# A decoder trunk on one core: the RWKV inverse on four 64x64 quadrants, rotary tables in steps, new mixing waits and a branch hint

## The chip, the cores and the metric

The kernel runs on one core of one Trainium2 chip. The metric is the device time of one execution in microseconds (us). The kernel before took 2006.41 us as the median of three runs (2005.33 to 2008.68). Engines are named as in the profile: PE (TensorE matmul) and PEld (its weight loads), DVE (VectorE), ACT (ScalarE), POOL (GpSimd) and SP (which issues the DMAs).

## The reference

The reference is a hybrid decoder trunk with two layers on 256 tokens of width 1024, in float32:

```
h = rmsnorm(x);  u = h @ W_in
x = x + (sum_m sigmoid(gate_m) * (mixer_m(u_m) @ P_m)) @ W_o      # SSD, NSA, RWKV-7, sliding-window attention
x = x + FFN(rmsnorm(x))          # layer 0: dense SwiGLU; layer 1: top-2 of 8 experts
x = x + sigmoid(x @ W_pg) * (p @ W_pp)
```

The RWKV mixer is a recurrence over tokens. For eight heads of size 64 it computes S_t = S_{t-1}(diag(w_t) - kk_t^T (a_t kk_t)) + v_t^T k_t and o_t = S_t r_t. The sliding-window mixer rotates its queries and keys by sine and cosine of position times frequency (rotary tables).

## The kernel before

**Main stream.** All large products go through one stream of units (`run_units`). A unit loads a piece of a weight from HBM (`raw`), splits it into a high part H (a cast on ACT, L318) and a low part L = raw - H (DVE, L321, and a quarter of the columns on POOL, L323), and then PE runs three matmuls for each product: H by H, L by H, H by L (L362 to L364). Results are called `fm` (features on partitions), `tokm` (tokens on partitions), `gu` and `dn` (expert layers).

**Side chains.** The mixers are Python generators (`rwkv_half`, `ssd`, `nsa`, `swa`, also `rope_tables` and `cast`). They are put on a list `side`, and each call of `tick` (L223), which stands between pieces of the main stream, lowers their counters; one whose counter has run out emits its instructions up to its next `yield`. How many ticks a step waits is read from the table `WAITS` by the generator's name and the step's number, else from the number that the generator yields. So WAITS decides where a chain's instructions stand among the main stream's. Nothing is reordered afterwards: every engine takes its instructions in the order in which they were emitted.

**The RWKV inverse.** Tokens are handled in chunks of 64. A "half" of the RWKV mixer (`rwkv_half`, four of them: two for each layer) has four heads and four chunks, 16 matrices of 64x64, held as 128 partitions by eight units: one matrix in partitions 0 to 63 and one in 64 to 127 of each unit. It needs the inverse of a unit triangular matrix for each, and builds it by doubling in five levels (L850 to L860). Level by level it forms `m1` = LO^T X (16 products, which the profile shows as 32 instructions, two for each float32 product), copies it to M1 on ACT, forms `dx` = XT^T M1 and `dxt` = M1^T XT, and adds them to X (L857) and to XT, the transpose of X (L859). The last level needs `dxt` alone. Each 64x64 product takes one quadrant of PE's 128x128 array: its rows are the partitions of the operands, its columns the partitions of the result. Before the change both are the same half, so the two products of a unit take the two quadrants on the diagonal:

```
ps = psb(name)
for u in range(8):
    for sl in HD:                                        # the two halves of the partitions
        mm(u3(ps)[sl, u], u3(lhs)[sl, u], rhs(sl, u), start=True, stop=True)
```

The start value X is a transpose of LO on PE (`d0`) plus the identity, and XT is LO plus the identity, made on POOL (L846). After the inverse a scan over four chunks follows (`rhs`, `sap`, `stp`, `op`); `sap` uses XT (L881).

**Rotary tables.** `rope_tables` (L518) emits ten POOL instructions in a row (L525 to L535), then waits once, then three on DVE (L537 to L539) and two on ACT. `cast` (L169) turns constants to bfloat16 on POOL.

**The branch.** The last part of the expert layer holds code for an expert with over 128 tokens. `tc.If(Z.most > P)` (L1996) lets every engine jump over it; with these inputs it is not needed. Behind the branch stands the scatter of the last expert (`last_scatter`, L1908): ACT casts yeH (L371), then PE forms `sct` (L1918).

Of the kernel before, what the change touches and what calls it, by code (L numbers as in the profile page):

```python
# [48 lines left out]
def _consts():  # L49
# [37 lines left out]
    for k, v in cols.items():  # L87
# [10 lines left out]


WAITS = {  # L100
# [19 lines left out]
}  # L120


def trunk_kernel(tc, I, out, dbg=None, upto=99):
# [38 lines left out]
    def late_consts(place):  # L162
        stages = []
        for c in range(NC32, NCST, 512):
            w = min(512, NCST - c)
            stages.append((c - NC32, w, place("stage")))
            nc.sync.dma_start(stages[-1][2][:, :w], I["consts"][:, c:c + w])

        def cast():  # L169
            yield 8.0  # L170
            for c, w, t in stages:
                nc.gpsimd.tensor_copy(cstb[:, c:c + w], t[:, :w])
        return cast

    def K(name):
        o, w = COFF[name]
        return cst[:, o:o + w] if o < NC32 else cstb[:, o - NC32:o - NC32 + w]
# [217 lines left out]
    def dma2(dst, src):  # L395
        nc.sync.dma_start(dst, src)
# [121 lines left out]
    def rope_tables(place):  # L518

        pool = nc.gpsimd  # L520
        pos, scr = place("pos"), place("scr")
        posi = pos.bitcast(I32)[:, 0:S]
        ang, nn = scr[:, 0:S], scr[:, S:2 * S]
        dma2(posi, I["positions"].to_broadcast([P, S]))
        pool.tensor_copy(ang, posi)  # L525
        pool.tensor_scalar(ang, ang, K("invf"), None, ALU.mult)
        magic = 12582912.0
        pool.tensor_scalar(nn, ang, 1.0 / (2 * math.pi), magic, ALU.mult, ALU.add)
        pool.tensor_scalar(nn, nn, magic, None, ALU.subtract)
        c1 = 6.28125  # L530
        c2 = 0.0019350051879882812
        c3 = 2 * math.pi - c1 - c2
        for c in (c1, c2, c3):
            pool.tensor_scalar(cosT, nn, -c, None, ALU.mult)
            pool.tensor_tensor(ang, ang, cosT, ALU.add)  # L535
        yield 12.0
        ts(ang, ang, math.pi, -math.pi, ALU.min, ALU.max)  # L537
        stt(nn, ang, -1.0, ang, ALU.mult, ALU.max)
        ts(nn, nn, -1.0, math.pi / 2, ALU.mult, ALU.add)  # L539
        yield 2.0  # L540
        act(sinT, ang, AF.Sin)
        act(cosT, nn, AF.Sin)
# [9 lines left out]
    def mixing(l, after):  # L552
# [176 lines left out]
        def rwkv_half(hf):  # L729
# [75 lines left out]
                        mm(u3(ps)[sl, u], u3(src)[sl, u], ident[sl, sl], start=True, stop=True)  # L805
                return ps

            def per_unit(lhs, rhs, name):
                ps = psb(name)
                for u in range(8):  # L810
                    for sl in HD:
                        mm(u3(ps)[sl, u], u3(lhs)[sl, u], rhs(sl, u), start=True, stop=True)
                return ps

            tok = []
            LT, Gka, Gbr, Gkr = (R(n) for n in ("LT", "Gka", "Gbr", "Gkr"))
            for src, da, dr in ((beta, LT, Gbr), (kap, Gka, Gkr)):
# [15 lines left out]
            bt, kpt, Vt = tok  # L833


            def off_diagonal(lev):
                LO = Z.mxr.tile([P, 512], F32, tag="LO", name="LO", bufs=2)
                nc.gpsimd.tensor_tensor(u3(LO), u3(LT), bmask("lv", lev * 64), ALU.mult)
                return LO
# [1 line left out]
            X, XT, M1 = R("X"), R("XT"), R("M1")  # L841
            LO = off_diagonal(0)
            yield
            ps = turn_units(LO, "d0")
            tt(u3(X), u3(ps), bmask("eye64"), ALU.add)
            nc.gpsimd.tensor_tensor(u3(XT), u3(LO), bmask("eye64"), ALU.add)  # L846
            LO = off_diagonal(1)
            yield
            for lev in range(1, 6):
                ps = per_unit(LO, lambda sl, u: u3(X)[sl, u], "m1")  # L850
                nc.scalar.copy(M1, ps)
                if lev < 5:
                    LO = off_diagonal(lev + 1)
                yield 1.6
                if lev < 5:
                    psx = per_unit(XT, lambda sl, u: u3(M1)[sl, u], "dx")
                    tt(X, X, psx, ALU.add)  # L857
                ps = per_unit(M1, lambda sl, u: u3(XT)[sl, u], "dxt")
                tt(XT, XT, ps, ALU.add)  # L859
                yield 2.2  # L860

# [2 lines left out]
            for c in range(4):  # L864
# [2 lines left out]
                    yield  # L867
                ps = psb("rhs")[:, :P]
                for q in range(2):
                    for sl in HD:  # L870
                        o = ps[sl, q * 64:q * 64 + 64]
                        mm(o, u3(Gka)[sl, u(q)], u3(Vt)[sl, u(q)], start=True, stop=c == 0)
                        if c:
                            mm(o, AR[sl, u(q), 0], St[sl, q], start=False, stop=True)
# [2 lines left out]
                yield  # L877
                ps = psb("sap")[:, :P]
                for q in range(2):
                    for sl in HD:  # L880
                        mm(ps[sl, q * 64:q * 64 + 64], u3(XT)[sl, u(q)], rh[sl, q], start=True, stop=True)  # L881
                sa = Z.mxr.tile([P, 2, 64], F32, tag="sa", name="sa", bufs=2)
                vec.tensor_copy(sa, ps.rearrange("p (q v) -> p q v", q=2))
                yield
# [491 lines left out]
        def swa():  # L1376
            mxa = Z.mxa
            qs = query_tile()
            ks = key_tile("kr")
            for n in range(5):  # L1380
                yield from until(F(f"rr{n}."))
                yield 2.0
                raw = rr[n]
                rp = psb("rotp")[:, :S]
                mm(rp, K("rot"), raw, start=True, stop=True)
                t = mxa.tile([P, S], F32, tag="rt", name="rtmp", bufs=2)
                tt(t, rp, sinT, ALU.mult)
                nc.gpsimd.tensor_tensor(raw, raw, cosT, ALU.mult)
                tt(t, t, raw, ALU.add)
                if n:  # L1390
                    split_to(qs[0][:, n - 1], qs[1][:, n - 1], t)
                else:
                    for g in range(2):
                        split_to(ks[0][HD[g], g], ks[1][HD[g], g], t[HD[g]])
            nsk = mxa.tile([P, 4, 2], F32, tag="nsk", name="nsk")
            ts(nsk, Z.snk.rearrange("p (g r) -> p r g", g=2), -1.0, None, ALU.mult)
            branch_out("swa", Z.mxa, 1)
            def use(PT, r):
                o = psb("so")[:, :S]
                pv(o, 256, PT, True, True)  # L1400
                head_out("swa", r, o)

            yield from until(F("nsa"))
            yield from attn_pipe([(qs, ks, r, None, True, nsk[:, r], lambda PT, r=r: use(PT, r)) for r in range(4)])
            flags.add(F("swa"))
# [329 lines left out]
    def moe(l, Z):  # L1735
# [252 lines left out]

        def load_most():
            Z.most = nc.values_load(Z.mxi[0:1, 0:1], min_val=0, max_val=S)  # L1990
            tc.mark_branch_hint_location("overflow")

        experts(0)

        def overflow():
            with tc.If(Z.most > P, label="overflow"):  # L1996
                keep = list(stream)
                stream.clear()
                experts(P)
                mine = list(stream)  # L2000
                stream[:] = keep
                with tc.tile_pool(name="ovr", bufs=2) as r2, tc.tile_pool(name="ovs", bufs=2) as s2:
                    run_units(mine, Slots(r2, 2, s2, 2))
            if f"xffn{l}" in dbg:
                for i in range(2):
                    nc.sync.dma_start(dbg[f"xffn{l}"][i], x[:, i])
# [44 lines left out]
```

## Time and profile before

| | |
|---|---|
| median of 3 runs | 2006.41 us (2005.33 to 2008.68) |
| profiled execution | 2005.13 us, of which the span is 2003.3 us |
| PE busy | 1938.6 us, 97% of the span |
| DVE, ACT, POOL busy | 77%, 59%, 56% |
| mean granted clock of PE | 0.989 |

Mixing takes about the first 440 us for layer 0 and from about 690 to 1117 us for layer 1; the dense layer lies between, the experts after. The page's "busy" of PE overlaps neighbouring matmuls, since they are pipelined; how long a group holds PE is read from the start of the group to the start of the next one.

### The profile page before, as it was taken

The numbers are of one execution on the slowest core, as the hardware profiler recorded it, in microseconds if no ns is written. First come the engines' busy times: TensorE is split into PE (matmuls) and PEld (weight loads), VectorE is DVE, ScalarE is ACT, GpSimd is POOL, SyncE is SP. The second block draws the span as 40 slices with busy tenths as digits, with TensorE's granted clock in tenths as the row PEclk, the third lists the DMA queues.
The fourth block names the chain that finished last, engine by engine and source line by source line (L and its number), as shares of the span: only waits on it lengthen the run. The fifth ranks groups of instructions, "written<-read, shape, count | busy, mean of one in ns | idle before, by whom it ended". The sixth has DMA issues, their size and how long they took to land. (4 is left out here: it accounts for less than half of the span.)

```text
span 2003.3 us, 37459 instructions
## 1 busy us (share of the span) xinstructions
PE 1938.6 (97%) x13236; PEld 1606.8 (80%) x13236; DVE 1533.7 (77%) x2432; ACT 1176.9 (59%) x1786; POOL 1120.4 (56%) x976
## 2 busy tenths in 40 slices
PE   7999999999999899999999999999999999999997
PEld 6798897778999788878777777778777877787775
DVE  6475756766555666656666589999999999999996
ACT  5333445545444443334455567777877787778773
POOL 4543254454555254414354666777767767777773
PEclk9999999999999999999999999999999999999998
DMA  7322464457665453228354889999999999999973
GB/s 202 96 75 82 111 146 137 117 160 216 187 189 166 115 133 93 76 85 163 102 146 137 280 270 354 313 330 351 360 354 331 347 362 357 328 349 362 354 255 107
DMA packets 419441, 435.78 MB, mean 218 GB/s; under 512 B 67876, under 2 KB 355624, under 8 KB 419240
## 3 DMA queue, kind: packets, MB, share of 16 engines
q1 hardware_dynamic: 419240, 433.26, 69.1%
q8 instruction: 106, 1.74, 0.4%
q14 instruction: 95, 0.78, 0.1%
HBM read 432.13 MB, written 1.05 MB: 216 GB/s over the span
## 5 line engine op out<-in xcount | busy, mean ns | idle before, releaser
L323 POOL TENSOR_TENSOR L<-raw,H 128x256 fp32r<-128x256 f32 (+1 forms) x794 | 950.8, 1207 | 808.7 <-ACT H L318 608.8
L321 DVE TENSOR_TENSOR L<-raw,H 128x768 fp32r<-128x768 f32 (+1 forms) x792 | 933.3, 1207 | 169.2 <-ACT H L318 166.7
L318 ACT CAST H<-raw 128x1024 fp32r<-128x1024 f32 x794 | 828.6, 1047 | 227.0 <-issue 44.8
L362 PE MATMUL gu<-H,GH 128*128 128x512 f32 x704 | 286.5, 407 | 0.1
L363 PE MATMUL gu<-L,GH 128*128 128x512 f32 x704 | 279.3, 397 | 0.5 <-DVE L L321 0.5
L364 PE MATMUL gu<-H,GL 128*128 128x512 f32 x704 | 278.1, 395 | 1.1 <-DVE GL L375 1.1
L364 PE MATMUL dn<-H,aL 128*128 128x512 f32 x440 | 173.9, 395 | 1.6 <-DVE aL L372 1.6
L363 PE MATMUL dn<-L,aH 128*128 128x512 f32 x440 | 174.5, 397 | 0.0
L362 PE MATMUL dn<-H,aH 128*128 128x512 f32 x440 | 174.3, 396 | 0.2 <-ACT pj L1576 0.2
L362 PE MATMUL fm<-hTH,H 128*128 128x256 f32 x560 | 166.9, 298 | 0.0
L363 PEld LDWEIGHTS gu<-L,GH 128*128 128x128 f32 x704 | 132.5, 188 | 41.1 <-DVE L L321 15.0
L363 PE MATMUL fm<-hTL,H 128*128 128x256 f32 x560 | 157.8, 282 | 0.0
L364 PE MATMUL fm<-hTH,L 128*128 128x256 f32 x560 | 157.5, 281 | 0.0
L364 PEld LDWEIGHTS gu<-H,GL 128*128 128x128 f32 x704 | 132.4, 188 | 29.0 <-DVE GL L375 2.7
L362 PEld LDWEIGHTS gu<-H,GH 128*128 128x128 f32 x704 | 132.3, 188 | 27.3 <-ACT GH L374 0.6
L362 PE MATMUL tokm<-H,hTH 128*128 128x512 f32 (+1 forms) x320 | 139.1, 435 | 4.4 <-ACT H L318 4.4
L363 PE MATMUL tokm<-L,hTH 128*128 128x512 f32 (+1 forms) x320 | 126.8, 396 | 5.6 <-POOL L L323 4.0
L364 PE MATMUL tokm<-H,hTL 128*128 128x512 f32 (+1 forms) x320 | 126.4, 395 | 0.0
L362 PEld LDWEIGHTS fm<-hTH,H 128*128 128x128 f32 x560 | 106.4, 190 | 5.9 <-issue 2.7
L363 PEld LDWEIGHTS fm<-hTL,H 128*128 128x128 f32 x560 | 106.4, 190 | 0.2
L364 PEld LDWEIGHTS fm<-hTH,L 128*128 128x128 f32 x560 | 106.2, 190 | 0.0
L363 PEld LDWEIGHTS dn<-L,aH 128*128 128x128 f32 x440 | 82.6, 188 | 23.8 <-DVE L L321 7.6
(507 smaller groups left out, 3520.2 us busy)
## 6 DMA issues: line engine op xcount, KB each, us to landing
raw<-moe_w_gate SPq DMA_DIRECT2D x341, 256.0 KB
raw<-moe_w_up SPq DMA_DIRECT2D x341, 256.0 KB
raw<-moe_w_down SPq DMA_DIRECT2D x169, 512.0 KB
raw<-w_in SPq DMA_DIRECT2D x126, 512.0 KB
raw<-ffn_w_gate SPq DMA_DIRECT2D x22, 512.0 KB
raw<-ffn_w_up SPq DMA_DIRECT2D x22, 512.0 KB
raw<-ffn_w_down SPq DMA_DIRECT2D x22, 512.0 KB
raw<-w_in SPq DMA_DIRECT2D x32, 256.0 KB
```

The costliest lines, as they stand in the source:

```text
L318: nc.scalar.copy(H[:, :n], raw[:, :n])
L321: tt(L[:, :m], raw[:, :m], H[:, :m], ALU.subtract)
L323: nc.gpsimd.tensor_tensor(L[:, m:n], raw[:, m:n], H[:, m:n], ALU.subtract)
L362: mm(o, l[0], r[0], start=start, stop=False)
L363: mm(o, l[0], r[1], start=False, stop=False)
L364: mm(o, l[1], r[0], start=False, stop=stop)
```

## The change

`m1` now goes to the other half of the columns, so M1 and XT lie in the partitions opposite to X. `dx` and `dxt` are emitted product by product in turn, so that a unit's four products name four different quadrants. `d0` is joined by `d0t`, a product with the identity as weights, which puts LO's copy in the other half; XT is then made on DVE from PSUM. `rhs` and `sap` follow the halves. The rotary tables, `cast` and `swa` have further `yield`s, and WAITS is set anew. The branch tests the opposite condition and has a hint.

```diff
 WAITS = {
+    'cast0': {0: 12, 1: 6, 2: 1, 3: 1, 4: 1},
+    'rope_tables0': {0: 10, 3: 7, 5: 3, 6: 4},
...
@@ rope_tables
         dma2(posi, I["positions"].to_broadcast([P, S]))
+        yield 2.5
         pool.tensor_copy(ang, posi)
         pool.tensor_scalar(ang, ang, K("invf"), None, ALU.mult)
+        yield 1.2
...
         for c in (c1, c2, c3):
             pool.tensor_scalar(cosT, nn, -c, None, ALU.mult)
             pool.tensor_tensor(ang, ang, cosT, ALU.add)
-        yield 12.0
+            yield 1.2
@@ rwkv_half
-            ps = turn_units(LO, "d0")
+            ps, pst = psb("d0"), psb("d0t")
+            for u in range(8):
+                for h, sl in enumerate(HD):
+                    mm(u3(ps)[sl, u], u3(LO)[sl, u], ident[sl, sl], start=True, stop=True)
+                    mm(u3(pst)[HD[1 - h], u], ident[sl, sl], u3(LO)[sl, u], start=True, stop=True)
             tt(u3(X), u3(ps), bmask("eye64"), ALU.add)
-            nc.gpsimd.tensor_tensor(u3(XT), u3(LO), bmask("eye64"), ALU.add)
+            tt(u3(XT), u3(pst), bmask("eye64"), ALU.add)
...
-                ps = per_unit(LO, lambda sl, u: u3(X)[sl, u], "m1")
+                        mm(u3(ps)[HD[1 - h], u], u3(LO)[sl, u], u3(X)[sl, u], start=True, stop=True)
...
+                psx = psb("dx") if lev < 5 else None
+                ps = psb("dxt")
+                for u in range(8):
+                    for h in range(2):
+                        if lev < 5:
+                            mm(u3(psx)[HD[h], u], u3(XT)[HD[1 - h], u], u3(M1)[HD[1 - h], u], start=True, stop=True)
+                        mm(u3(ps)[HD[1 - h], u], u3(M1)[HD[1 - h], u], u3(XT)[HD[1 - h], u], start=True, stop=True)
                 if lev < 5:
-                    psx = per_unit(XT, lambda sl, u: u3(M1)[sl, u], "dx")
                     tt(X, X, psx, ALU.add)
-                ps = per_unit(M1, lambda sl, u: u3(XT)[sl, u], "dxt")
                 tt(XT, XT, ps, ALU.add)
@@ swa
                 tt(t, t, raw, ALU.add)
+                yield 1.2
                 if n:
                     split_to(qs[0][:, n - 1], qs[1][:, n - 1], t)
@@ load_most, overflow
-            tc.mark_branch_hint_location("overflow")
+            tc.mark_branch_hint_location("overflow", "LikelyTaken", engines=list(mybir.ALL_ENGINES))
-            with tc.If(Z.most > P, label="overflow"):
+            with tc.If(Z.most <= P, label="overflow", preferred_fallthrough_block=False) as fits:
+                pass
+            with fits.Else():
```

On PE, at a level of the first half, the kernel before runs one product kind after the other (16 source products each):

```order
L362 MATMUL fm<-hTH,H 128x256
L363 MATMUL fm<-hTL,H 128x256
L364 MATMUL fm<-hTH,L 128x256
L812 MATMUL dx<-M_828,XT 64x64 x16
L812 MATMUL dxt<-XT,M_828 64x64 x16
L362 MATMUL fm<-hTH,H 128x256
```

The changed kernel has the same 32 in turn; six of them with the main matmuls ahead:

```order
L368 MATMUL fm<-hTH,H 128x256
L369 MATMUL fm<-hTL,H 128x256
L370 MATMUL fm<-hTH,L 128x256
L870 MATMUL dx<-M_814,XT 64x64
L871 MATMUL dxt<-XT,M_814 64x64
L870 MATMUL dx<-M_814,XT 64x64
L871 MATMUL dxt<-XT,M_814 64x64
L870 MATMUL dx<-M_814,XT 64x64
L871 MATMUL dxt<-XT,M_814 64x64
```

The number of main matmuls ahead of a level is the same at most levels; only the turn within the group is new.

On POOL, in layer 0 where the rotary tables are made, the kernel before has all ten instructions ahead of a low part L that the main stream needs (`kp`, `AR` and `kap` belong to RWKV):

```order
L775 TENSOR_TENSOR kp<-kp,k 128x512
L781 TENSOR_TENSOR AR<-r,Dd 128x8x64
L525 CAST scr<-pos 128x256
L526 TENSOR_SCALAR scr<-scr,cst 128x256
...
L534 TENSOR_SCALAR cosT<-scr 128x256
L535 TENSOR_TENSOR scr<-scr,cosT 128x256
L323 TENSOR_TENSOR L<-raw,H 128x192
L787 TENSOR_TENSOR kap<-kp,inv 128x512
L323 TENSOR_TENSOR L<-raw,H 128x192
```

The changed kernel puts four low parts ahead and spreads the rest:

```order
L784 TENSOR_TENSOR kp<-kp,k 128x512
L790 TENSOR_TENSOR AR<-r,Dd 128x8x64
L796 TENSOR_TENSOR kap<-kp,inv 128x512
L329 TENSOR_TENSOR L<-raw,H 128x192 x2
L329 TENSOR_TENSOR L<-raw,H 128x256 x2
L532 CAST scr<-pos 128x256
L533 TENSOR_SCALAR scr<-scr,cst 128x256
L841 TENSOR_TENSOR LO<-LT,cstb 128x512
L536 TENSOR_SCALAR scr<-scr 128x256
L537 TENSOR_SCALAR scr<-scr 128x256
L329 TENSOR_TENSOR L<-raw,H 128x256
```

On ACT, in layer 0 where `swa` rotates its queries (`qTH`, from `rtmp`) beside the softmax of `nsa` (`Pm`), the kernel before has two such casts close together, the second straight ahead of a cast H of the main stream:

```order
L371 CAST qTH<-rtmp 128x256
L1145 ACTIVATE Pm,ls<-sc,nm 128x256 x2
L1368 ACTIVATE rraw<-fm 128x256
L371 CAST qTH<-rtmp 128x256
L318 CAST H<-raw 128x1024
L1368 ACTIVATE rraw<-fm 128x256
```

In the changed kernel the second one has moved behind four casts H and a softmax:

```order
L377 CAST qTH<-rtmp 128x256
L1160 ACTIVATE Pm,ls<-sc,nm 128x256 x2
L1383 ACTIVATE rraw<-fm 128x256
L324 CAST H<-raw 128x1024 x3
L1160 ACTIVATE Pm,ls<-sc,nm 128x128 x2
L324 CAST H<-raw 128x1024
L377 CAST qTH<-rtmp 128x256
```

Every engine's stream has the hint (`BRANCH_PREFETCH_HINT`) as its first instruction of the kernel proper, not beside the branch.

## Rows read from the trace of the kernel before

**Rows 1.** Page, part 1: engine, busy us (share of span), instructions.
```profile
PE 1938.6 (97%) x13236; PEld 1606.8 (80%) x13236; DVE 1533.7 (77%) x2432; ACT 1176.9 (59%) x1786; POOL 1120.4 (56%) x976
```
**Rows 2.** Waits of PE: for whom, total us, times, longest us.
```profile
PE tokm L362 <- ACT H L318: 4.4, 2, 3.3
PE tokm L363 <- POOL L L323: 4.0, 2, 3.6
PE sct L1918 <- ACT yeH L371: 3.5, 1, 3.5
PE bop L797 <- DVE bq L792: 3.1, 3, 1.8
...
PE m L812 <- DVE X L857: 0.8, 1, 0.8
```
**Rows 3.** Windows: stretch, length, busy us by engine, PEclk, DMA share, GB/s.
```profile
70.00:170.00 100.00, 98.97 (x1657) 89.45 (x1654) 66.96 (x141) 40.80 (x68) 41.61 (x33) 1.00 0.29 82
59.00:62.00 3.00, 3.00 (x19) 2.46 (x20) 0.00 (x0) 0.00 (x0) 1.96 (x3) 0.50 0.81 197
302.10:306.00 3.90, 3.69 (x10) 2.70 (x11) 3.65 (x4) 2.12 (x3) 3.81 (x3) 0.50 0.31 80
1963.00:1967.00 4.00, 3.47 (x11) 2.37 (x12) 2.20 (x4) 0.43 (x1) 0.00 (x0) 0.53 0.29 94
```
**Rows 4.** Timeline of PE, one level: start us, us, operation [idle before].
```profile
78.38 1.15 PE L812 MATMUL m<-X,LO 64*64 64x64 f32 x32
79.46 0.39 PE L362 MATMUL fm<-hTH,H 128*128 128x256 f32 x1
...
83.40 1.15 PE L812 MATMUL dx<-M,XT 64*64 64x64 f32 x32
84.39 1.10 PE L812 MATMUL dxt<-XT,M 64*64 64x64 f32 x32
85.42 0.39 PE L362 MATMUL fm<-hTH,H 128*128 128x256 f32 x1
```
**Rows 5.** PE, tile dx: count, ns min/median/max, first and last start.
```profile
L812 PE MATMUL dx<-M,XT x512: 218/218/267, 83.4 to 840.7; 64*64 64x64 f32 x171
```
**Rows 6.** Timeline of PE: a row half, then two column halves.
```profile
75.33 0.38 PE L737 MATMUL lwp<-lora,lor 64*128 64x256 f32 x1
...
75.54 0.38 PE L737 MATMUL lwp<-lora,lor 64*128 64x256 f32 x1
...
329.96 0.66 PE L1201 MATMUL no<-PT,vtok 128*64 128x256 f32 x4
...
330.66 0.65 PE L1201 MATMUL no<-PT,vtok 128*64 128x256 f32 x4
```
**Rows 7.** Timeline of PE, the scan's state products.
```profile
150.63 0.22 PE L892 MATMUL stp<-St,cst 64*64 64x64 f32 x1
150.63 0.27 PE L890 MATMUL stp<-tok 64*64 64x64 f32 x1
...
150.75 0.22 PE L893 MATMUL stp<-sa,tok 64*64 64x64 f32 x1
```
**Rows 8.** Timeline of DVE at the inverse's start.
```profile
74.22 0.69 DVE L845 TENSOR_TENSOR X<-d,cstb 128x512 f32<-128x512 f32 x1 [0.89 <-PE d L805]
```
**Rows 9.** Timeline of POOL and of PE where the rotary tables stand.
```profile
48.13 0.60 POOL L525 CAST scr<-pos 128x256 f32<-128x256 int32 x1 [0.94 <-DMA pos<-positions]
...
57.91 0.59 POOL L323 TENSOR_TENSOR L<-raw,H 128x192 fp32r<-128x192 f32 x1
...
58.55 0.72 PE L363 MATMUL tokm<-L,hTH 128*128 128x416 f32 x1 [3.64 <-POOL L L323]
```
**Rows 10.** Timeline of ACT and of PE behind the branch.
```profile
1961.79 0.58 ACT L371 CAST yeH<-dn 128x512 fp32r<-128x512 f32 x1 [5.09 <-PEq L1996]
...
1962.43 0.49 PE L1918 MATMUL sct<-yeH,OHT 128*128 128x512 f32 x1 [3.50 <-ACT yeH L371]
```
**Rows 11.** Timeline of ACT, query rotation in layer 0.
```profile
300.71 0.40 ACT L371 CAST qTH<-rtmp 128x256 fp32r<-128x256 f32 x1 [1.67 <-DVE rtmp L1389]
```

More of the change, by code (lines that the diff above doesn't have):

```diff
@@ L172, in cast @@
                 nc.gpsimd.tensor_copy(cstb[:, c:c + w], t[:, :w])
+                yield
         return cast
@@ L806, in turn_units @@
                 return ps
[L808 to L813, printed above, removed]
             tok = []
@@ L849, in rwkv_half @@
             for lev in range(1, 6):
-                ps = per_unit(LO, lambda sl, u: u3(X)[sl, u], "m1")
+                ps = psb("m1")
+                for u in range(8):
+                    for h, sl in enumerate(HD):
+                        mm(u3(ps)[HD[1 - h], u], u3(LO)[sl, u], u3(X)[sl, u], start=True, stop=True)
                 nc.scalar.copy(M1, ps)
@@ L854, in rwkv_half @@
                 yield 1.6
+                psx = psb("dx") if lev < 5 else None
+                ps = psb("dxt")
+                for u in range(8):
+                    for h in range(2):
+                        if lev < 5:
+                            mm(u3(psx)[HD[h], u], u3(XT)[HD[1 - h], u], u3(M1)[HD[1 - h], u], start=True, stop=True)
+                        mm(u3(ps)[HD[1 - h], u], u3(M1)[HD[1 - h], u], u3(XT)[HD[1 - h], u], start=True, stop=True)
                 if lev < 5:
-                    psx = per_unit(XT, lambda sl, u: u3(M1)[sl, u], "dx")
                     tt(X, X, psx, ALU.add)
-                ps = per_unit(M1, lambda sl, u: u3(XT)[sl, u], "dxt")
                 tt(XT, XT, ps, ALU.add)
@@ L869, in rwkv_half @@
                 for q in range(2):
-                    for sl in HD:
-                        o = ps[sl, q * 64:q * 64 + 64]
+                    for h, sl in enumerate(HD):
+                        o = ps[HD[1 - h], q * 64:q * 64 + 64]
                         mm(o, u3(Gka)[sl, u(q)], u3(Vt)[sl, u(q)], start=True, stop=c == 0)
@@ L879, in rwkv_half @@
                 for q in range(2):
-                    for sl in HD:
-                        mm(ps[sl, q * 64:q * 64 + 64], u3(XT)[sl, u(q)], rh[sl, q], start=True, stop=True)
+                    for h in range(2):
+                        mm(ps[HD[h], q * 64:q * 64 + 64], u3(XT)[HD[1 - h], u(q)], rh[HD[1 - h], q], start=True, stop=True)
                 sa = Z.mxr.tile([P, 2, 64], F32, tag="sa", name="sa", bufs=2)
@@ L1389, in swa @@
                 tt(t, t, raw, ALU.add)
+                yield 1.2
                 if n:
```

35 rows, old and new, of the table WAITS are left out of this document.

## Prediction

> **What bounds the kernel now.** I read the page's busy times first: PE is busy for 1938.6 us of a span of 2003.3, no other engine above 77% [rows 1]. So nearly every microsecond that PE no longer works comes off the time, if the stage in which it is saved is PE's too. The windows answer that: in 100 us of layer 0's mixing, where the inverses stand, PE is busy for 98.97, DVE for 66.96, ACT and POOL for about 41, and the DMA share is 0.29 [rows 3]. There a shorter PE group makes all that follows earlier. Then I read the waits of PE, to see which of the remaining gaps the change can reach [rows 2], and for each the timeline at its place [rows 9 to 11]. Last I looked at the granted clock behind these gaps. It is 0.50 to 0.53 of full, the 1.2 GHz level instead of 2.4, from 59 to 62 us, from 302.1 to 306 and from 1963 to 1967 [rows 3], each time after PE had stood for over 3 us [rows 2, 9, 10].
>
> **Term 1: dx and dxt on four quadrants.** One level holds PE from 83.40 to 85.42, 2.02 us for 64 instructions, while m, 32 instructions on two quadrants, holds it from 78.38 to 79.46, 1.08 us [rows 4]. So two quadrants on the diagonal already work side by side: an instruction of 256 columns holds its part of the array for 0.21 us (75.33 to 75.54 [rows 6]), one of 64 columns by that for a quarter, 0.053, and 32 one after another would take 1.7 us; 16 for each quadrant fit. The change gives four quadrants 16 instructions each. If they all run side by side, the level takes as long as m plus a little for issuing more: I take 1.09, a gain of 0.93. Dx has 512 instructions [rows 5], 32 for each level, so there are 16 such levels: 16 x 0.93 = 14.9 us. The fifth level of each half has dxt alone, on two quadrants as before, and m, rhs and sap stay at two: no change there.
>
> Can quadrants with the same rows work side by side? The kernel has no 64x64 case of it, but a near one. In pv two products of 128 rows use the column halves. Pv has four instructions of 256 columns and four of 128, which by the same 0.21 us one after another would take 4 x 0.21 + 4 x 0.105 = 1.26 us; from 329.96 to 330.66 it took 0.70 [rows 6]. So two column halves over the same rows, with different data, do overlap, as row halves do. Bounds for the term: 0, if the four work as two pairs, and 15.0 (16 x 0.94), if the longer group costs nothing at all. By the nearest rows I take 14.9.
>
> D0 gets d0t, 32 more instructions on the two free quadrants, four times: 0 by the same rows, 4 x 0.94 = 3.8 us lost if they don't overlap. XT there moves from POOL to DVE, 0.69 us as for X [rows 8], four times 2.8 us of DVE, which has a third of that stretch free [rows 3]: 0. If that cover were gone, the next m would wait for X or XT; the trace shows one such wait, 0.8 us [rows 2].
>
> **A rule that speaks against term 1.** The state products of the scan are emitted six instructions at a time for one partition half (L890, L892, L893, two each), then for the other. On PE an L890 starts together with the first half's L892 at 150.63, before that half's L893 at 150.75 [rows 7]: the second half's instructions overtake the first half's. The Trainium skill, page "TensorE: Matmul & The Clock Gate", section "Packing small matmuls" ("The mechanism"), says that matmuls are "pc-monotone in start AND end — strict FIFO, no reordering". By that rule the second of a product's two instructions holds up all that is behind it, and the sum would be rival 1's; by the rows it is 14.9. The rows decide here, and no run yet shows four quadrants.
>
> **Term 2: the rotary tables.** From 48.13 POOL is given ten instructions in a row; the low part that PE's next main matmul needs starts at 57.91, and PE waits 3.64 us [rows 9]. In the changed order four low parts and kap stand ahead of the tables, and the rest is in pieces between further low parts. That wait goes: 3.6. Behind it PE works for 3.0 us at clock 0.50 [rows 3], which at 1.0 is half: 1.5 more. What is late next there is bop, which waits 1.8 us for bq on DVE [rows 2]; it stays, as its place moves by one main product only. Term 2 is 5.1 us; bounds 0 (another piece of POOL's work ahead of an L) and 6.9 (the bop wait goes too).
>
> **Term 3: the branch.** PE waits 3.50 us for yeH, and ACT's cast of yeH waits 5.09 for PE's sequencer at the If, L1996 [rows 10]. The jump is what holds them. If the hint hides it, what is left is the cast itself (1961.79 to 1962.43, 0.64) and the wake-up behind the last dn, about 0.15 by estimate: 0.8. That gives 3.5 - 0.8 = 2.7 us. The stretch behind runs at 0.53 with PE busy for 3.47 of 4 us [rows 3]; at full clock that saves up to 1.7, and I take 1.5, since DVE and ACT hold part of it. Term 3 is 4.2. No row shows a hint at work, and it stands two milliseconds ahead of its branch, so the lower bound is 0; the upper is 3.5 + 1.7 = 5.2.
>
> **Term 4: query rotation in layer 0.** PE waits 3.3 us once for a cast H [rows 2]. ACT had stood 1.67 us on a query cast whose input came late from DVE, with that H behind it [rows 11]. The new yield in swa lets that cast be emitted a step after its input, and the second query cast now stands behind four H. The wait goes, 3.3, and of the 3.69 us that PE was busy at 0.50 behind it [rows 3] half: 5.2 in all. Bounds: 0, if the wait moves to another H, and 5.2.
>
> The other new waits move chain steps by a few main products each way. Their gaps of before are under 1.1 us apiece; I count them at 0, with 4 us either way as an estimate from the sum of such waits. The extra yields of cast and tables cost no instruction.
>
> **Sum.** 14.9 + 5.1 + 4.2 + 5.2 = 29.4 us off the profiled execution's 2005.13 gives 1975.7. That execution stands 1.3 under the median of the three runs, so for a median I add 1.3: 1977.0. A change within 0.2% (4 us) cannot be told from none here.
>
> **Rivals.**
> 1. *In-order issue.* The two instructions of one product stand next to each other, so if PE takes instructions strictly in turn, only the second of one and the first of the next overlap, and 64 instructions take 32 times 0.06 to 0.065, the 2.02 of now. For it: the pairs of before would look alike under this rule. Against it: rows 7. Term 1 is 0, and the time 2006.4 - 14.5 = 1992.
> 2. *The gap moves into the chain.* X is now added after dx and dxt instead of beside dxt, so the next m may wait for DVE. For it: one m waited 0.8 us for X [rows 2]. Against it: in the level of rows 4, m of the next level starts 3 us behind. If each of the 16 levels waited as long as that one, it would cost 16 x 0.8 = 12.8, and the time would be 1990.
> 3. *The hint does nothing*, so the change does not do what it says there: the engines reach the old code over the same jump. Term 3 is 0 and the time 1981.
> 4. *Slower: a drain at every change of columns.* Place: between two products of dx and dxt that share rows. Price: entering and leaving the 64x64 group costs 1.08 - 16 x 0.058 (150.63 to 150.75 holds two intervals, so 0.058 to 0.06 each [rows 7]) = 0.15 us together, about 0.08 a change. With 31 changes on top of 32 products in series a level takes about 1.9 + 2.5 = 4.4 us, 2.4 more than now; over 16 levels 38 us, and four d0 groups some 12. Less the 14.5 of terms 2 to 4 that is 2006.4 + 35.5 = 2042. It decides once a level takes over 2.02 + 14.5/20 = 2.75 us. Against it: pv changes columns four times over in its 0.70 us [rows 6].
>
> **How the numbers follow.** The forecast has 0.64, with a range of its own from 1968 to 1986: 4 us of other waits either way, 1.8 for bop below, and one of terms 2 to 4 failing above (up to 5.2). Rival 1 has 0.12, rival 2 0.10, rival 3 0.10, rival 4 0.04. The range from 1966 to 1992 takes in the forecast's own range and rivals 1 to 3, and leaves out rival 4 and the tails. Faster by over 0.2%: 0.94; within 0.2%: 0.02, if two of the rivals meet; slower: 0.04.
>
> **What the changed profile would show.** Term 1: the start of a dx group to the next main matmul is 1.1 us, with dx and dxt starting together; about 2.0 would be rival 1, over 2.75 rival 4. Term 2: no wait of PE for POOL's L near 58 us, and clock 1.0 behind it. Term 3: sct waits under 1 us for yeH; 3.5 would be rival 3. Term 4: no 3 us wait of tokm for H near 300 us. Rival 2 would show as waits of m for X, several times over. Wrong altogether: waits of PE that add up to more than before in places that I have not named, or DVE over 90% busy where the inverses stand.

## The result, and the profile after

The changed kernel took 1976.76 us as the median of four runs (1975.06 to 1978.64); the kernel before, beside it, 2005.87 (2004.78 to 2008.68). The ratio is 0.9856 with a 95% interval of 0.9843 to 0.9868: 28.9 us less, where 29.4 had been forecast. The profiled execution took 1978.64 us with a span of 1976.9. The total is right to half a microsecond, and that is luck: of its four terms only one lies inside the interval that was measured for it, two are 5.8 us too high together and one 5.4 too low.

The page, part 1, of the changed kernel (engine, busy us, share, instructions), which answers to [rows 1]:

```profile
PE 1918.5 (97%) x13364; PEld 1591.3 (80%) x13364; DVE 1532.0 (77%) x2436; ACT 1178.2 (60%) x1786; POOL 1115.2 (56%) x972
```

PE is still the bound: it lost 20 us of work, the span 26. Its waits, to be read against [rows 2] (total us, times, longest; bop is an RWKV product that needs bq from DVE, trp a transpose):

```profile
PE bop L806 <- DVE bq L801: 6.6, 4, 3.9
PE m L860 <- DVE X L873: 2.9, 2, 1.7
PE trp L1531 <- DVE x L1498: 2.8, 2, 2.6
...
PE sct L1934 <- ACT yeH L377: 0.8, 1, 0.8
...
PE tokm L369 <- POOL L L329: 0.4, 1, 0.4
```

Gone are the waits for the cast H (4.4 us), for POOL's L (3.6 of 4.0) and most of the branch's (3.5 to 0.8). Grown are bop's (3.1 to 6.6) and m's for X (0.8 to 2.9): rival 2, in small. The trp wait is 2.6 us here and 1.4 in runs of the changed kernel below with the same code there, so nothing is read from it.

A level of the inverse on PE in the changed kernel (start us, length, operation), beside [rows 4]:

```profile
80.43 0.27 PE L870 MATMUL dx<-M,XT 64*64 64x64 f32 x1
80.43 0.27 PE L871 MATMUL dxt<-XT,M 64*64 64x64 f32 x1
80.44 0.27 PE L870 MATMUL dx<-M,XT 64*64 64x64 f32 x1
80.45 0.27 PE L871 MATMUL dxt<-XT,M 64*64 64x64 f32 x1
80.53 0.22 PE L870 MATMUL dx<-M,XT 64*64 64x64 f32 x1
...
80.59 0.22 PE L870 MATMUL dx<-M,XT 64*64 64x64 f32 x1
...
81.37 0.22 PE L871 MATMUL dxt<-XT,M 64*64 64x64 f32 x1
81.52 0.39 PE L368 MATMUL fm<-hTH,H 128*128 128x256 f32 x1
```

Four instructions start within 0.02 us, and from 80.53 on four more every 0.058 us: 64 in 1.09 us (80.43 to 81.52), where they took 2.02. That is term 1 as it was worked out.

Windows of the changed kernel (stretch, length, busy us by engine, PEclk, DMA share, GB/s), beside [rows 3]:

```profile
70.00:170.00 100.00, 96.82 (x1717) 85.68 (x1710) 72.02 (x148) 43.65 (x74) 47.41 (x43) 1.00 0.31 92
51.00:57.50 6.50, 5.96 (x24) 3.89 (x24) 3.54 (x6) 0.00 (x0) 0.20 (x1) 0.50 0.59 163
278.00:300.00 22.00, 22.00 (x134) 18.96 (x133) 16.60 (x35) 11.65 (x26) 9.27 (x9) 1.00 0.49 145
```

Where the inverses stand PE is now idle for 3.2 us in 100 and DVE busier (67 to 72): the stage has come nearer to DVE. The half clock near 300 us is gone, the one behind bop is still there.

### The profile page after: what moved, and what is told of

It is laid out like the page before. It is cut to its first block, busy times and chain, and to the rows that moved or that the text cites. A ratio compares the mean times of both kernels' runs of the same rounds, so it can differ in the third digit from the quotient of the medians.

```text
span 1976.9 us, 37722 instructions
## 1 busy us (share of the span) xinstructions
PE 1918.5 (97%) x13364; PEld 1591.3 (80%) x13364; DVE 1532.0 (77%) x2436; ACT 1178.2 (60%) x1786; POOL 1115.2 (56%) x972
```

## The experiments

Times are medians; ratios are to the kernel before, run in turn with each, with 95% intervals. The kernel before took 2005.7 to 2007.4 us beside them, so where two experiments are compared, the difference of their ratios is given too.

**1. The quadrants alone.** Before, with the new inverse:

```
-                ps = per_unit(LO, lambda sl, u: u3(X)[sl, u], "m1")      # and dx, dxt, d0, rhs, sap
+                        mm(u3(ps)[HD[1 - h], u], u3(LO)[sl, u], u3(X)[sl, u], start=True, stop=True)
```

> The kernel before with the change to the RWKV inverse alone (m1 into the other half, dx and dxt in turn, d0 with d0t, rhs and sap following); all waits, tables, swa and the branch as before. Theory (four quadrants work side by side, PE bounds that stage, the gain needs none of the new waits): a dx+dxt group goes from 2.01 to 1.09 us in all 16 levels, 16 x 0.92 = 14.7 us, so 2005.9 - 14.7 = 1991 (range 1988 to 1994). Rival A (the gain is only there because the new waits leave the next m its time): m waits for X at several levels, 0.8 us or more each, and the time is 1996 or more. Rival B (a good part of the 29 us comes from the inverse by another way than the group's length, as by the clock): under 1986.

1997.0 us, ratio 0.9958 (0.9944 to 0.9971): 8.4 us of the 14.7. The groups take 1.09 us, so the gain was made on PE and given back as waits, as rival A says, though not by m alone. PE's waits in this run:

```profile
PE bop L797 <- DVE bq L792: 4.7, 4, 2.0
...
PE m L851 <- DVE X L864: 3.2, 2, 1.7
...
PE stp L899 <- DVE sa L889: 1.5, 1, 1.5
```

In [rows 2] bop had 3.1 us, m 0.8; stp waits for sa 0.5 us in the kernel before. Together these waits grew by 5.0 of the 6.3 us.

**2. Dx ahead of dxt.** The changed kernel, with the order of before in the new quadrants:

```
+                if lev < 5:
+                    for u in range(8):
+                        for h in range(2):
+                            mm(u3(psx)[HD[h], u], ...)          # all of dx
+                for u in range(8):
+                    for h in range(2):
+                        mm(u3(ps)[HD[1 - h], u], ...)           # then all of dxt
```

> The changed kernel with all 16 products of dx emitted ahead of all 16 of dxt, each still in its new quadrant; nothing else differs. Theory (what pays is that neighbours in the order name four different quadrants; each quadrant takes its own instructions in order and only a few instructions can wait ahead of a busy one): the group takes 2.0 us again and the time is 1976.8 + 14.7 = 1991.5 (1988 to 1995). Rival (PE can reach over 32 instructions to the free quadrants, so the order is of no account): the group stays at 1.1 us and the time at 1977. In between, if dxt starts some rounds before dx is done: the number of dxt instructions that start before the last dx shows how far PE reaches.

1983.91 us, ratio 0.9888 (0.9873 to 0.9903): 7.2 above the changed kernel, 6.4 by the ratios. The group takes 1.84 us, not 2.0; the timeline of PE shows why:

```profile
81.16 0.97 PE L870 MATMUL dx<-M,XT 64*64 64x64 f32 x26
81.92 0.27 PE L873 MATMUL dxt<-XT,M 64*64 64x64 f32 x2
81.97 0.28 PE L870 MATMUL dx<-M,XT 64*64 64x64 f32 x3
...
82.09 0.22 PE L870 MATMUL dx<-M,XT 64*64 64x64 f32 x1
82.09 0.98 PE L873 MATMUL dxt<-XT,M 64*64 64x64 f32 x27
83.00 0.39 PE L368 MATMUL fm<-hTH,H 128*128 128x256 f32 x1
```

The first two dxt start when 26 of 32 dx have started: they pass over the six that still wait for their busy quadrants. So PE does not start its products strictly in turn, but reaches only a few instructions ahead; "every engine takes its instructions in the order in which they were emitted", in the part on the kernel before, does not hold for these starts on PE. The order in which products are emitted is what fills the quadrants. 16 x 0.75 = 12 us were lost on PE, 7.2 in time: here too some 0.6 of a microsecond counts. The waits of bop for bq and of m for X are 1.9 us shorter in this trace than in the changed kernel's (5.4 and 2.2 against 6.6 and 2.9), so a longer group covers waits; what the rest is was not shown.

**3. The tables alone.** Before, with the steps of `rope_tables` and `cast` and their two rows of WAITS.

> The kernel before with the rotary tables and the cast of constants in steps and their two rows of waits; nothing else. Theory (the long wait of PE for POOL's low part at 58.5 us goes, but kap and the low parts on POOL now run beside DVE's beta and bq, which take 1.65 instead of 0.88 and 1.0 us, so bop starts near 51.5 instead of 51.0): POOL's L wait 3.64 goes to under 0.6, bop's wait grows from 1.82 to about 2.5, with the clock 2 to 4 us less: 2002 to 2004. Rival (as predicted blind: bop's wait in the changed kernel grew only because bop stands earlier on PE, and DVE isn't slowed): bop waits 1.8 here, betas and bq take 0.88 and 1.0, and 5 us are gained: 2000.8. Rival 2: the pieces end up ahead of another low part and nothing is gained: 2006.

2003.39 us, ratio 0.9988 (0.9979 to 0.9997): 2.4 us, as the theory says. PE's long wait for L is gone, and bop, at the same place among the main products as before, waits 3.42 us instead of 1.82:

```profile
53.25 2.07 PE L803 MATMUL bop<-bq,cst 128*128 128x512 f32 x2 [3.42 <-DVE bq L798]
```

DVE ahead of bop, in the kernel before and then in this one:

```profile
47.66 0.81 DVE L321 TENSOR_TENSOR L<-raw,H 128x640 fp32r<-128x640 f32 x1
48.39 0.88 DVE L785 SCALAR_TENSOR_TENSOR beta<-beta,kkn 128x512 f32<-128x512 f32 x1
49.20 0.81 DVE L321 TENSOR_TENSOR L<-raw,H 128x640 fp32r<-128x640 f32 x1
49.93 1.01 DVE L792 SCALAR_TENSOR_TENSOR bq<-r,par,kp 128x256 f32<-128x256 f32 x2
```

```profile
47.91 1.21 DVE L324 TENSOR_TENSOR L<-raw,H 128x640 fp32r<-128x640 f32 x1
49.05 1.76 DVE L791 SCALAR_TENSOR_TENSOR beta<-beta,kkn 128x512 f32<-128x512 f32 x1
50.73 1.21 DVE L324 TENSOR_TENSOR L<-raw,H 128x640 fp32r<-128x640 f32 x1
51.86 1.34 DVE L798 SCALAR_TENSOR_TENSOR bq<-r,par,kp 128x256 f32<-128x256 f32 x2
```

The same four groups take 3.51 and 5.52 us. What differs is POOL beside them: table work of one input before, products of two inputs now. POOL in this run, the first row beside DVE's first L, the second beside beta, the third beside the rest:

```profile
47.40 1.04 POOL L326 TENSOR_TENSOR L<-raw,H 128x192 fp32r<-128x192 f32 x1
48.40 1.86 POOL L793 TENSOR_TENSOR kap<-kp,inv 128x512 f32<-128x512 f32 x1
50.22 2.30 POOL L326 TENSOR_TENSOR L<-raw,H 128x192 fp32r<-128x192 f32 x2
```

DVE does not work at a lower rate here, it waits for POOL's operation to end: L ends 0.68 us behind POOL's L (48.44 to 49.12), beta 0.55 us behind kap (50.26 to 50.81), and with POOL idle operations of their forms take 0.81 and 0.69. The other traces say the same: of some 5700 L of 128x768 that DVE began while a two-input operation of POOL had over 0.2 us left, nine in ten ended 0.81 to 0.82 us behind that operation's end, however long it still ran; an L that DVE began first took 0.96, and 0.95 with POOL idle. Of POOL's table work the cast held beta up in the same way (0.88 in the kernel before), the scalar operation beside the second L did not (0.81). POOL waits as well: its L took 1.04 us, begun while a beta of DVE was still under way, where the L of [rows 9] took 0.59.

Behind bop the clock is as low as it was. In the kernel before it is 0.51 and 0.50 from 51.7 to 55.1 and from 58.6 to 62.0 us; in this run (stretch, length, busy us by engine, PEclk, DMA share, GB/s):

```profile
51.90:58.70 6.80, 5.45 (x22) 3.56 (x23) 3.61 (x7) 0.00 (x0) 0.61 (x1) 0.50 0.74 193
```

**4. The sliding window alone.** Before, with the new `yield` in `swa` and the new waits of swa and nsa.

> The kernel before with the new yield in swa and the new waits of swa0, swa1, nsa0 and nsa1; nothing else. Theory: the wait of 3.3 us for H near 300 us goes and with it the half clock of 6.8 us behind it, 5.2 us; in layer 1 the gaps of 1.0 and 0.5 us near 984 and the 3.4 us of half clock behind them belong to the same chains and go too, 3.2 us: 2005.9 - 8.4 = 1997.5. If layer 1's gap is another chain's: 2000.7. Rival (the gap moves to another H, since the softmax of nsa and the casts of swa need the same ACT): a wait of tokm or fm for H of 2 us or more elsewhere, and 2004 to 2007.

1995.36 us, ratio 0.9947 (0.9934 to 0.9961): 10.6 us. Both stretches count; the `yield` and the new waits were not tried apart. Windows of the kernel before, and then of this one:

```profile
300.90:307.70 6.80, 5.39 (x14) 4.03 (x15) 4.84 (x8) 4.13 (x9) 4.53 (x4) 0.50 0.39 105
987.00:990.40 3.40, 3.40 (x11) 2.40 (x10) 2.30 (x7) 0.84 (x1) 2.14 (x2) 0.50 0.52 159
```

```profile
294.00:304.00 10.00, 10.00 (x58) 8.39 (x57) 7.28 (x15) 5.98 (x13) 3.62 (x3) 1.00 0.46 111
970.00:980.00 10.00, 10.00 (x51) 7.86 (x50) 7.79 (x18) 5.69 (x15) 2.96 (x3) 1.00 0.42 113
```

**5. The quadrants with the chains' new waits.** Experiment 1 with the rows of WAITS of rwkv_half0 to 3, ssd0 and ssd1.

> The kernel before with the change to the RWKV inverse and the new waits of the four rwkv_half chains and of ssd0 and ssd1; tables, cast, swa, nsa and the branch as before. The quadrants alone brought 8.7 us where 14.7 were worked out from the groups' length, and PE stood 5 us more in the two stretches of the inverses (sa 1.5, m for X 1.7 and 1.5, bop 1.4). Theory (the new waits of these chains are what keeps the 14.7: they put main matmuls back where the shorter groups had taken the cover from DVE's work): 2005.7 - 14.7 = 1991, and under 2 us of m, sap and stp waits in the inverses. Rival (the loss has another cause, such as DVE and POOL having the same work in less time, which waits can't mend): 1996 to 1998.

1995.07 us, ratio 0.9941 (0.9927 to 0.9954): 11.8 us, between theory and rival, with the theory at the very edge of the interval. Counting the 7944 main matmuls in both traces, the 4680th (behind layer 1's mixing) starts 13.7 us earlier than in the kernel before, against 9.7 us in experiment 1; the 4 us are all won in layer 0. In this execution sct then waited 5.2 us behind the branch, 1.7 more than in [rows 2], which no part of the edit touches.

**6. The waits alone.** The same rows of WAITS with the old inverse.

> The kernel before with the new waits of rwkv_half0 to 3, ssd0 and ssd1 and nothing else: the other half of the comparison with the quadrants. Theory (these waits are worth nothing by themselves, they only fit the shorter groups): 2005.7 within 2 us. Rival A (they bring their 5 us with the old groups too, so they are a gain apart from the quadrants): 2000 to 2002. Rival B (they fit only the new lengths, and cost with the old): 2009 or more.

2008.33 us, ratio 1.0009 (1.0000 to 1.0018). They bring nothing by themselves. Beside the shorter groups they are worth 3.4 us by the ratios of experiments 1 and 5, whose intervals overlap, and 4.0 by the two traces. They also move bop three main matmuls forward, where it waits longer, with the tables as before:

```profile
50.15 1.62 PE L798 MATMUL bop<-bq,cst 128*128 128x512 f32 x2 [2.99 <-DVE bq L793]
```

**7. The branch alone.** Before, with the opposite condition and the hint.

> The kernel before with the branch's opposite condition and its hint, nothing else. Theory (the hint hides the jump): sct waits 0.8 instead of 3.5 us, the half-clock stretch behind it shrinks from 6.8 to 3.4 us or goes, and 2005.7 - 4 = 2001.7 (2000.5 to 2003). Rival (the gain came with the earlier arrival of the whole tail, not with the branch): 2005.7.

2001.29 us, ratio 0.9972 (0.9961 to 0.9982): 5.6 us, the theory's 4 inside the interval. The wait of sct is 0.8 us.

**8. No hint.** The changed kernel with

```
-            tc.mark_branch_hint_location("overflow", "LikelyTaken", engines=list(mybir.ALL_ENGINES))
+            tc.mark_branch_hint_location("overflow")
```

> The changed kernel without the hint; the branch's condition stays the opposite one, with the old code in its else part. Theory (it is the hint that does it): sct waits 3.5 us again for yeH, and 1976.8 + 4 = 1980.8 (1979 to 1982). Rival (it is the condition, since the engines now take the branch over the old code another way): sct stays at 0.8 us and the time at 1977.

1980.58 us, ratio 0.9871 (0.9856 to 0.9887): 3.8 above the changed kernel, 3.0 by the ratios, whose intervals overlap; the waits settle it. ACT and PE behind the branch, without the hint and then with it (the changed kernel):

```profile
1936.91 0.59 ACT L377 CAST yeH<-dn 128x512 fp32r<-128x512 f32 x1 [5.86 <-DVEq L2012]
1937.54 0.79 PE L1934 MATMUL sct<-yeH,OHT 128*128 128x512 f32 x1 [4.38 <-ACT yeH L377]
```

```profile
1935.49 0.58 ACT L377 CAST yeH<-dn 128x512 fp32r<-128x512 f32 x1 [2.63 <-PEq L2012]
1936.13 0.49 PE L1934 MATMUL sct<-yeH,OHT 128*128 128x512 f32 x1 [0.81 <-ACT yeH L377]
```

So the hint does it, and the opposite condition by itself does not; the hint with the old condition was not tried. With no hint the wait varies: 3.5 us [rows 2], 4.2 (experiment 4), 4.4, 5.2 (experiment 5).

**9. Turns of two units.** The changed kernel with four products of dx, then four of dxt, in turn.

> The changed kernel with the turns between dx and dxt twice as long as a whole unit: four products of dx (two units), then the four of dxt, and so on. When all of dx stood ahead of all of dxt, the first dxt started while six instructions of dx had not started. Theory (PE passes over about six waiting instructions, so a turn of eight is still covered): the first dxt starts with the first dx or one round of 0.058 us later, and the group takes 1.1 to 1.25 us; time 1977 to 1979. Rival (the four quadrants pay only if neighbours in the order name four different ones): 1.4 to 1.84 us for the group, and by what 1.84 cost before (7 us) 1980 to 1984.

1978.03 us, ratio 0.9856 (0.9838 to 0.9874): the changed kernel's. The group takes 1.14 us, and the first dxt start 0.03 us behind the first dx:

```profile
80.36 0.27 PE L871 MATMUL dx<-M,XT 64*64 64x64 f32 x2
80.39 0.27 PE L874 MATMUL dxt<-XT,M 64*64 64x64 f32 x2
80.47 0.23 PE L871 MATMUL dx<-M,XT 64*64 64x64 f32 x2
```

Each product is two instructions, so the first dxt stands behind eight of dx, two of which run: six again. Neighbours need not name different quadrants; the next free one must stand within that reach.

**10. One half of the rows first.** The changed kernel with `for h` outside `for u`.

> The changed kernel with all products of dx and dxt that read the one half of the partitions ahead of all that read the other: neighbours in the order share their rows of PE and differ in the columns alone. Theory (two column halves over the same rows work side by side, as any two quadrants, and the seam overlaps by six instructions): the group takes 1.84 us, as with dx ahead of dxt, and the time is 1984 (1981 to 1987). Rival A (column halves over the same rows hold each other up when nothing else runs): 2.5 to 3.7 us for the group, 16 levels, and 1990 to 2010. Rival B (the seam differs, since both quadrants of the second half must wait for none): under 1.5 us and 1979.

1987.72 us, ratio 0.9904 (0.9886 to 0.9922). The group takes 1.84 us, as the theory says:

```profile
79.09 0.27 PE L870 MATMUL dx<-M,XT 64*64 64x64 f32 x1
79.10 0.27 PE L871 MATMUL dxt<-XT,M 64*64 64x64 f32 x1
79.20 0.22 PE L870 MATMUL dx<-M,XT 64*64 64x64 f32 x1
79.20 0.22 PE L871 MATMUL dxt<-XT,M 64*64 64x64 f32 x1
...
80.93 0.39 PE L368 MATMUL fm<-hTH,H 128*128 128x256 f32 x1
```

Two column halves over the same rows run side by side at the full rate, as pv had it [rows 6]. The expected time was 3.7 us short, for the most part because this order also runs the fifth level's dxt on one quadrant after another: 1.73 to 1.83 us, from the first dxt to what follows the last, instead of 0.98 to 1.13, four times, about 2.9 us. That I had not counted.

**11. A mended version.** The changed kernel with other waits:

```
-    'rwkv_half0': {..., 10: 4, ..., 15: 3, 16: 4, ..., 24: 2, 25: 6, ...}
+    'rwkv_half0': {..., 10: 7, 11: 1, ..., 15: 2, 16: 3, ..., 24: 5, 25: 3, ...}     # half1, half2 alike
```

> The changed kernel with some waits of rwkv_half0, 1 and 2 set so that bop stands 9, 18 and 6 main products later, the fifth m 18 later in the first half of each layer, and all else where it was. PE waits there 3.9, 1.4 and 1.1 us for bq and 1.25 and 1.7 us for X now, 9.3 us together, and one half-clock stretch of 6.8 us follows the first. Theory (main products are at hand to cover these waits): the waits of m go under 0.4, those of bop fall by half or more; the first is bound by DVE's low part, which is done at 49.9 where bop started at 51.5, so about 2 us stay there. 5 to 6 us of waits and up to 3 of clock: 1969 to 1972. Rival (DVE is what is late there, and the main products ahead of bop wait for its low part as bop did): the gaps get other names, and 1975 to 1978.

1970.75 us, ratio 0.9819 (0.9805 to 0.9832), 6.0 below the changed kernel, 7.4 by the ratios. The waits for bq no longer stand among PE's waits of 0.5 us or more; instead PE waits where the theory left it, for DVE's low part, and still twice for X:

```profile
PE m L855 <- DVE X L868: 2.4, 2, 1.7
...
PE tokm L364 <- DVE L L322: 2.0, 1, 2.0
PE tokm L364 <- POOL L L324: 1.8, 2, 1.3
```

The 1.7 us are layer 1's fourth m, not the fifth that I had moved.

**12. Two more waits.** The mended version with that m 18 main products later, and DVE's low part ahead of the second beta.

> The mended kernel with two more waits set: the fourth m of layer 1's first half stands 18 main products later (it still waited 1.7 us for X, which stands on DVE behind AR and beta of the other half), and in layer 0 DVE makes the low part that PE waits for (2.05 us) ahead of the second beta instead of behind it. Theory: the m wait goes, 1.7 us. The low part is done near 48.7 instead of 50.3, but bop's bq stays where it was on DVE (51.9), so what PE gains on the low part it loses on bop but for 0.5 us: 2.2 us in all, 1968.5 (1967 to 1970). Rival (the sum of waits is DVE's, and m's wait moves on to the next step): no gain, 1970.7. [...]

1970.96 us, ratio 0.9825 (0.9811 to 0.9838): no gain, as the rival has it. That wait of m for X is gone, and the next step of the other half takes its place:

```profile
760.74 1.10 PE L801 MATMUL bop<-bq,cst 128*128 128x512 f32 x2 [1.89 <-DVE bq L796]
```

In layer 0 bop waits again too, 1.5 us for bq. At both places DVE is what is late, and these two moves of the order brought nothing.

## Why the prediction was right in its total and wrong in three terms

**Term 1 (forecast 14.9, measured 11.8, 9.2 to 14.7).** The mechanism and the size on PE are as forecast: 16 x 0.93, four quadrants at the rate of two. Rival 1 is out, by the groups of 1.09 us and by the rows of experiments 2 and 9: instructions overtake others. The Trainium skill's rule, page "TensorE: Matmul & The Clock Gate", section "Packing small matmuls" ("The mechanism"), that matmuls are "strict FIFO, no reordering", does not hold for the starts of these 64x64 products. The step that failed is "There a shorter PE group makes all that follows earlier", by which PE's gain was counted in full: without the new waits 5 to 6 us of it return as waits for DVE (experiment 1), with them 1.0 by the trace up to the 4680th main matmul and about 3 by the medians (experiment 5). Rival 2 is true in part, in two places instead of 16. D0t cost nothing on PE, as forecast: d0 with d0t takes 1.09 us, d0 alone took 1.08.

**Term 2 (forecast 5.1, measured 2.4, 0.6 to 4.2).** The step that failed is "it stays, as its place moves by one main product only", said of bop's wait. POOL's L wait went, 3.6 us, but bop's grew from 1.8 to 3.9, for two reasons. The one main product, three matmuls, is no small thing: with the new waits alone bop waits 3.0 (experiment 6). And I looked at bop's place on PE and not at what DVE does meanwhile: with the tables out of the way, kap and three low parts run on POOL just beside beta and bq, and DVE takes 2 us longer for them, so that bop waits 3.4 with the tables alone (experiment 3). The Trainium skill, page "GPSIMD Engine Reference", section "1. Specifications", lists the contention of GpSimd with VectorE instructions that have two SBUF inputs; the rows of experiment 3 agree, 0.88 to 1.76 us for beta. The 1.5 us for the clock failed with it: bop's longer gap has 6.8 us at 0.50 behind it, as long as the two stretches of before together, and only PE's busy time in them fell, from 6.6 to 5.45 us, which at that clock is worth 0.6.

**Term 3 (forecast 4.2, measured 3.0 to 3.8 by experiment 8 and 5.6, 3.6 to 7.8, by experiment 7).** Right: 0.8 us of sct's wait was forecast and measured. The clock behind it is 1.00 from 1959 to 1967 us in experiment 7; in the changed kernel's profile a stretch at 0.50 is left from 1938.3 to 1941.7, half as long as in the kernel before (6.8 us), so the 1.5 us put down for the clock varies with the execution. Rival 3 is out.

**Term 4 (forecast 5.2, measured 10.6, 7.8 to 13.2).** The mechanism holds; the term was mis-sized three times. I took 3.9 us of half clock behind the gap where the window shows 6.8 with PE busy for 5.39, so 2.7 us instead of 1.9. And [rows 2] had two waits for H, 4.4 us together, of which I used the longest alone: the other, in layer 1, and the 3.4 us at half clock behind it belong to the same chains, 1.0 + 1.7. That gives 3.3 + 2.7 + 1.0 + 1.7 = 8.7, and 0.5 for a second small gap there. The third is that four more waits of these chains, of 0.9, 0.8 and twice 0.4 us, were put at 0 among the other waits, and they are gone in experiment 4 too; with them it is 11.7, against the measured 10.6. The 1.7 is the least certain: only three of the six traces that have the gap of 1.0 us in layer 1 have a half clock behind it.

**The other waits** were put at 0 with 4 us either way. They hold losses that here stand in other terms: bop's 1.4 near 105 us and 0.9 more on an m of layer 1 in term 1's shortfall (experiments 1 and 5 have them), an m's 1.25 near 109 us in term 2's (experiment 3 has it, and experiments 1 and 5 do not). The lower end of the forecast's own range does not come out of its parts either: 1977.0 - 4 - 1.8 is 1971, not 1968. The four parts, each by itself, give 11.8 + 2.4 + 5.6 + 10.6 = 30.4; together they gave 28.9, so they add up within their intervals. Rival 4, the drain, is out: no group took longer than before.

What stays open: how far the trp wait near 1120 us (1.4 or 2.6) and the length of a half-clock stretch behind the same gap vary from run to run, which is a few microseconds in any comparison of single traces.

## What to carry to other kernels

Lay operands and results out so that the products name different quadrants, and emit them so that the next free quadrant stands within some six instructions: then they run side by side. When work on the bounding engine gets shorter, the waits that it covered come up; set the side chains anew and measure the two together, since here the new waits alone brought nothing and the shorter groups alone little more than half of their gain. Read a wait's row for its count as well as its longest, and before POOL is given other work, look at what DVE does at that moment.

## What the runs showed of the hardware

- PE passes over about six waiting 64x64 instructions to reach a free quadrant (experiments 2 and 9), and four quadrants each take an instruction every 0.058 us.
- An operation of DVE with two inputs that begins while a two-input one of POOL is under way ends a fixed time behind it (L of 128x768 0.82 us, beta 0.55), however much of it was left. In experiment 3 this made L 1.21 us instead of 0.81 and beta 1.76 instead of 0.88. POOL's L, begun under an operation of DVE, took 1.04 us instead of 0.59.
- With a branch hint at the program's start, sct behind a jump 1.9 ms later waited 0.8 us in all seven traces that have the hint, and 3.5 to 5.2 us in the seven that have not.
